# Row-wise absolute maximum of an 8192 x 8192 matrix: loads split over two DMA queues, joins gathered into one, last result transposed on the tensor engine

## Chip, cores and metric

The kernel runs on one core of one Trainium2 chip. The metric is device time in microseconds (us) from launch to end of one execution; lower is better. Before the change the median of 10 runs is 631.82 us (631.76 to 632.32).

## Reference

```python
x = np.random.randn(8192, 8192).astype(np.float32)

def reference(x):
    return np.linalg.norm(x, ord=np.inf, axis=1)
```

The reference takes, for each row of x, the largest absolute value of 8192 float32 numbers. The input is 268.4 MB, the output 32 KB. There is no arithmetic beyond one maximum for each element.

## The kernel before

The 8192 rows of x are handled as 64 "rows" of 128 partitions: one such row is 128 x 8192 numbers (4 MB), one x-row per partition. From here on "row" means such a block of 128 x-rows, and a "pair" is two of them, loaded by one instruction as 128 x 16384 (8 MB).

`PIECES` lists the loads, unit by unit: four single rows (`HEAD`), 23 whole pairs, five pairs cut into pieces, three single rows cut into pieces, and the last row cut into six pieces that shrink from 1984 to 832 columns. Pairs are numbered 1 to 28 here, in the order of loading: pairs 1 to 23 are whole, pair 24 is two loads of 8192, pairs 25 to 28 are cut unevenly. All loads are issued by SyncE (SP, line 106), and land in one buffer, `ring`, of three pairs' width (`RING`); only the last piece has a buffer of its own (`last`). The place in the ring goes round, so pair n lies where pair n-3 lay: its load may start only when VectorE has reduced pair n-3.

VectorE (DVE) does all the reducing (`absmax`, line 58), in the order of the loads. A piece that holds a whole row goes straight to a column of `res`; pieces of rows go to columns of `part`, and `join` (line 63) takes the maximum of a row's columns once they are all there. A join is held back by one reduction (`pending`), so it never stands directly behind the reduction whose result it needs. There are eight joins.

The results stand one per partition, and the output needs them along a line. Rows of results are therefore transposed on TensorE (lines 71 and 82), copied out of PSUM by ScalarE (ACT, lines 72 and 83) and stored from ACT's DMA queue (lines 73 and 84): the four heads once they are first possible, the 28 pairs after the first cut single row, the three single rows near the end. The very last row goes another way: its reduction `fin` (line 108) fills column 0 of a 128 x 32 tile, VectorE transposes that in blocks of 32 x 32 (line 144), and SP stores four lines of 32 numbers (line 145).

The Tile layer that records the kernel adds the semaphore waits and decides, within each engine, in which order instructions stand. DMA completions are counted on eight semaphores, here called lanes 0 to 7, that are given out in turn.

Of the kernel before, what the change touches and what calls it, by code (L numbers as in the profile page):

```python
# [1 line left out]

# [5 lines left out]

P = 128
FP32 = mybir.dt.float32  # L10
MAX = mybir.AluOpType.max

HEAD = 4
PAIRS = 28
PIECES = (
    [[8192]] * HEAD
    + [[16384]] * 23  # L20
    + [[8192, 8192], [12288, 4096], [8960, 7424], [8704, 7680], [5504, 6016, 4864]]
    + [[4288, 3904], [3072, 2752, 2368], [2240, 2112, 1984, 1856]]
    + [[1984, 1664, 1472, 1152, 1088, 832]]
)
RING = 3 * 16384


@with_exitstack
def kernel(
    ctx: ExitStack,  # L30
    tc: tile.TileContext,
    x: bass.AP,
    out: bass.AP,
):
    nc = tc.nc
    n_rows, n_cols = x.shape
    R = n_rows // P
    assert R == 64 and n_cols == 8192

    single = ctx.enter_context(tc.tile_pool(name="single", bufs=1))  # L40
    psum_pool = ctx.enter_context(tc.tile_pool(name="psum", bufs=1, space=bass.MemoryType.PSUM))

    ring = single.tile([P, RING], FP32)
    res = single.tile([P, R], FP32)
    part = single.tile([P, R, 8], FP32)
    ident = single.tile([P, P], FP32)
    make_identity(nc, ident)


    n_last = len(PIECES[-1]) - 1  # L50
    w_last = PIECES[-1][-1]
    last = single.tile([P, w_last + n_last], FP32)
    fin = single.tile([P, 32], FP32)
    fin_t = single.tile([P, 32], FP32)
    nc.gpsimd.memset(fin, 0.0)  # L55

    def absmax(dst, src):
        nc.vector.tensor_reduce(  # L58
            out=dst, in_=src, axis=mybir.AxisListType.X, op=MAX, apply_absolute_value=True,
        )  # L60

    def join(row, n):
        nc.vector.tensor_reduce(  # L63
            out=res[:, row : row + 1], in_=part[:, row, :n], axis=mybir.AxisListType.X, op=MAX,
        )

    def rows_out(r0, n):

        ps = psum_pool.tile([n, P], FP32, name=f"ps{r0}")
        sb = single.tile([n, P], FP32, name=f"sb{r0}")  # L70
        nc.tensor.transpose(ps, res[:, r0 : r0 + n], ident)  # L71
        nc.scalar.copy(sb, ps)  # L72
        nc.scalar.dma_start(
            out=out[r0 * P : (r0 + n) * P].rearrange("(r p) -> r p", p=P), in_=sb
        )

    def pairs_out():
        sb = single.tile([PAIRS, P, 2], FP32, name="sb_pairs")
        both = res[:, HEAD : HEAD + 2 * PAIRS].rearrange("p (g r) -> p g r", r=2)
        for r in range(2):  # L80
            ps = psum_pool.tile([PAIRS, P], FP32, name=f"ps_pairs{r}")
            nc.tensor.transpose(ps, both[:, :, r], ident)  # L82
            nc.scalar.copy(sb[:, :, r], ps)  # L83
        nc.scalar.dma_start(
            out=out[HEAD * P : (HEAD + 2 * PAIRS) * P].rearrange("(g p r) -> g p r", p=P, r=2),
            in_=sb,
        )

    at = 0
    row = 0  # L90
    pending = None
    for u, widths in enumerate(PIECES):
        k = sum(widths) // n_cols
        src = x[row * P : (row + k) * P].rearrange("(p r) m -> p (r m)", r=k)
        off = 0
        n_part = {}
        for h, w in enumerate(widths):
            final = u == len(PIECES) - 1 and h == n_last
            if final:
                buf = last[:, :w]  # L100
            else:
                if at + w > RING:
                    at = 0
                buf = ring[:, at : at + w]
                at += w
            nc.sync.dma_start(out=buf, in_=src[:, off : off + w])
            if final:
                absmax(fin[:, :1], last)
                break
            s = 0  # L110
            while s < w:
                r = row + (off + s) // n_cols
                left = n_cols - (off + s) % n_cols
                if left == n_cols and w - s >= n_cols:
                    c = (w - s) // n_cols
                    absmax(
                        res[:, r : r + c],
                        buf[:, s : s + c * n_cols].rearrange("p (c m) -> p c m", m=n_cols),
                    )
                    s += c * n_cols  # L120
                    continue
                e = min(w, s + left)
                i = n_part.get(r, 0)
                n_part[r] = i + 1
                if r == R - 1:
                    absmax(last[:, w_last + i : w_last + i + 1], buf[:, s:e])
                else:
                    absmax(part[:, r, i : i + 1], buf[:, s:e])

                if pending is not None:  # L130
                    join(*pending)
                    pending = None
                if e - s == left and r < R - 1:
                    pending = (r, i + 1)
                s = e
            off += w
        row += k
        if row == HEAD + 2 * PAIRS + 1:
            pairs_out()
            rows_out(0, HEAD)  # L140
    assert pending is None
    rows_out(HEAD + 2 * PAIRS, R - 1 - HEAD - 2 * PAIRS)

    nc.vector.transpose(fin_t, fin)  # L144
    nc.sync.dma_start(
        out=out[(R - 1) * P :].rearrange("(b c) -> b c", c=32), in_=fin_t[0:P:32, :]
    )
    assert row == R


# [1 line left out]
_INS = ['x']  # L152
_OUTS = [((8192,), 'float32')]


# [23 lines left out]
```

## Time and profile before

| | before |
|---|---|
| median of 10 runs | 631.82 us |
| the profiled execution | 631.78 us |
| its span (first to last instruction) | 630.0 us |
| VectorE busy | 553.5 us (88%) |
| HBM read | 268.44 MB, 426 GB/s over the span |
| TensorE, ScalarE, GpSimd busy | 1.5, 2.3, 0.8 us |

The span is 1.8 us shorter than the time of the same execution. All instants below are microseconds from the start of the span. In rows of the profile, `res<-ring 128x2 f32<-128x16384 f32` is an instruction that reads a tile of 128 partitions by 16384 numbers in `ring` and writes 128 x 2 numbers to `res`; `SPq` rows are the time in which SP's queue was issuing loads or waiting to.

### The profile page before, as it was taken

What the parts mean: (1) busy time and instruction counts of PE and PEld (TensorE: products, weight loads), DVE (VectorE), ACT (ScalarE), POOL (GpSimd) and SP (SyncE); (2) the same over time, 40 slices, a digit from 0 to 9 for tenths busy, and PEclk for the clock granted to TensorE, in tenths of its full rate; (3) what the DMA queues carried; (4) which work ended last, traced back from release to release, by engine and by line L of the source; (5) the groups of instructions that cost most, each with busy time, mean ns of one, the idle gap of its engine ahead of it and who ended that gap; (6) DMA issues with size and microseconds to landing.
All of it is one profiled execution on the core that took longest, in us unless ns stands there. A gap on an engine that the chain in (4) does not pass through costs nothing. (4 is left out here: it accounts for less than half of the span.)

```text
span 630.0 us, 225 instructions
## 1 busy us (share of the span) xinstructions
PE 1.5 (0%) x4; PEld 0.4 (0%) x4; DVE 553.5 (88%) x66; ACT 2.3 (0%) x5; POOL 0.8 (0%) x7
## 2 busy tenths in 40 slices
PE   0000000000000000000000000000000000000000
PEld 0000000000000000000000000000000000000000
DVE  1983988889988889888899888898888999999998
ACT  0000000000000000000000000000000000000000
POOL 0000000000000000000000000000000000000000
DMA  8999999999999999999999999999999999999995
GB/s 370 435 460 420 445 424 441 445 420 449 416 454 412 466 399 466 399 466 399 466 399 466 399 466 399 466 399 466 399 466 399 433 433 424 447 416 428 425 421 237
DMA packets 7698, 268.49 MB, mean 426 GB/s; under 512 B 877, under 2 KB 912, under 8 KB 1936
## 3 DMA queue, kind: packets, MB, share of 16 engines
q1 hardware_dynamic: 7640, 268.44, 98.9%
q10 hardware_dynamic: 56, 0.03, 0.0%
q14 instruction: 2, 0.02, 0.0%
HBM read 268.44 MB, written 0.03 MB: 426 GB/s over the span
## 5 line engine op out<-in xcount | busy, mean ns | idle before, releaser
L58 DVE TENSOR_REDUCE res<-ring 128x2 f32<-128x16384 f32 (+1 forms) x32 | 473.9, 14818 | 73.5 <-DMA ring<-in_x_dram 73.5
L58 DVE TENSOR_REDUCE part<-ring 128x1 f32<-128x4096 f32 (+17 forms) x19 | 70.0, 3735 | 0.0
L58 DVE TENSOR_REDUCE last<-ring 128x1 f32<-128x1984 f32 (+4 forms) x5 | 8.1, 1678 | 0.0
L83 ACT COPY sb_pairs<-ps_pairs 28x128 f32<-28x128 f32 x2 | 0.5, 262 | 540.1 <-PE ps_pairs L82 540.1
L82 PE MATMUL ps_pairs<-ident,res 128*28 128x128 f32 x2 | 0.8, 396 | 539.8 <-DVE res L63 539.8
L63 DVE TENSOR_REDUCE res<-part 128x1 f32<-128x2 f32 (+2 forms) x8 | 1.2, 154 | 0.2
L72 ACT ACT_TABLE_LOAD x1 | 1.3, 1283 | 0.7 <-PEq L163 0.7
L58 DVE TENSOR_REDUCE fin<-last 128x1 f32<-128x837 f32 x1 | 1.0, 1025 | 0.1
L71 PE MATMUL ps<-ident,res 128*4 128x128 f32 (+1 forms) x2 | 0.7, 372 | 77.1 <-DVE res L58 50.8
L72 ACT COPY sb<-ps 4x128 f32<-4x128 f32 (+1 forms) x2 | 0.5, 254 | 75.6 <-PE ps L71 75.6
L82 PEld LDWEIGHTS ps_pairs<-ident,res 128*28 128x28 f32 x2 | 0.2, 104 | 540.4 <-DVE res L63 540.4
masks.py:199 POOL TENSOR_SCALAR_AFFINE_SELECT ident<-ident 128x128 f32<-128x128 f32 x1 | 0.3, 292 | 0.0
L144 DVE STREAM_TRANSPOSE fin_t<-fin 128x32 f32<-128x32 f32 x1 | 0.2, 211 | 0.0
L71 PEld LDWEIGHTS ps<-ident,res 128*4 128x4 f32 (+1 forms) x2 | 0.2, 82 | 77.4 <-issue 50.8
masks.py:197 POOL MEMSET ident<- 128x128 f32 x1 | 0.2, 204 | 0.3 <-POOLq L163 0.3
L55 POOL MEMSET fin<- 128x32 f32 x1 | 0.1, 125 | 0.0
L163 POOL MEMSET const-bfloat16-1.0<- 128x1 bf16 x1 | 0.1, 101 | 0.0
L163 POOL MEMSET const-uint8-127<- 128x1 uint8 x1 | 0.1, 101 | 0.0
L163 POOL MEMSET const-float32-0.0<- 128x1 f32 x1 | 0.1, 98 | 0.2 <-issue 0.2
L163 POOL MEMSET const-float32-1.0<- 128x1 f32 x1 | 0.1, 98 | 0.0
## 6 DMA issues: line engine op xcount, KB each, us to landing
ring<-in_x_dram SPq DMA_DIRECT2D x6, 4096.0 KB, 30.9
ring<-in_x_dram SPq DMA_DIRECT2D x1, 6144.0 KB, 36.1
ring<-in_x_dram SPq DMA_DIRECT2D x1, 4480.0 KB
ring<-in_x_dram SPq DMA_DIRECT2D x1, 4352.0 KB, 34.2
ring<-in_x_dram SPq DMA_DIRECT2D x1, 3840.0 KB
ring<-in_x_dram SPq DMA_DIRECT2D x1, 3712.0 KB
ring<-in_x_dram SPq DMA_DIRECT2D x1, 3008.0 KB
ring<-in_x_dram SPq DMA_DIRECT2D x1, 2752.0 KB, 41.3
```

Of the source, the lines that this page charges most:

```text
L55: nc.gpsimd.memset(fin, 0.0)
L58: nc.vector.tensor_reduce(out=dst, in_=src, axis=mybir.AxisListType.X, op=MAX, apply_absolute_value=True,)
L63: nc.vector.tensor_reduce(out=res[:, row : row + 1], in_=part[:, row, :n], axis=mybir.AxisListType.X, op=MAX,)
L71: nc.tensor.transpose(ps, res[:, r0 : r0 + n], ident)
L72: nc.scalar.copy(sb, ps)
L82: nc.tensor.transpose(ps, both[:, :, r], ident)
L83: nc.scalar.copy(sb[:, :, r], ps)
L144: nc.vector.transpose(fin_t, fin)
L163: nc = _bacc.Bacc("TRN2", target_bir_lowering=False, num_devices=1)
```

## The change

- The first 24 loads (4 heads and pairs 1 to 20) stay on SP; pairs 21 to 28, the three single rows and the last row are issued by ScalarE (ACT). On ACT, all these loads stand ahead of the copies and stores. Every load is put behind what its own engine already has (`keep_in_program_order`).
- Rows are renumbered: pairs take rows 0 to 55 of x, the seven single rows (the four heads included) rows 56 to 62. One transpose, one copy and one store serve the seven.
- All rows from number 48 (`CUT`) on have four columns in `part` (15 x 4 columns), and those not written by a reduction are zeroed beforehand. One instruction joins all 15 rows, directly before the last row.
- The pieces of pairs 25 to 28, of the three single rows and of the last row have other widths; their number is unchanged.
- The zeroing of `part`, and the building of the identity matrix, now wait until the first row is reduced. They were ahead of it.
- The last row's result is transposed on TensorE, copied out of PSUM by VectorE and stored by SP as one line of 128 numbers.

```diff
-    + [[8192, 8192], [12288, 4096], [8960, 7424], [8704, 7680], [5504, 6016, 4864]]
-    + [[4288, 3904], [3072, 2752, 2368], [2240, 2112, 1984, 1856]]
-    + [[1984, 1664, 1472, 1152, 1088, 832]]
+    + [[8192, 8192], [7232, 9152], [6720, 9664], [8640, 7744], [5568, 5568, 5248]]
+    + [[4480, 3712], [3392, 1920, 2880], [2752, 1600, 2048, 1792]]
+    + [[1792, 1664, 1472, 1280, 1088, 896]]
 )
+SP_PAIRS = 20
+CUT = 48
+K = 4
...
+    def setup(after):
+        for ins in (nc.gpsimd.memset(part[:, :, 1:], 0.0), nc.gpsimd.memset(ident, 0.0)):
+            tc.add_manual_dep(
+                ins.ins, after.name,
+                mybir.DependencyInfo(mybir.DependencyClass.Sync, mybir.DependencyReason.DATA),
+                reason="not before the first row is in",
+            )
+        make_identity(nc, ident, nomemset=True)
...
+        if k == 2:
+            row, next_pair = next_pair, next_pair + 2
+        else:
+            row, next_one = next_one, next_one + 1
...
-            nc.sync.dma_start(out=buf, in_=src[:, off : off + w])
+            queue = nc.sync if u < HEAD + SP_PAIRS else nc.scalar
+            tc.keep_in_program_order(
+                queue.dma_start(out=buf, in_=src[:, off : off + w])
+            )
...
-                if pending is not None:
-                    join(*pending)
-                    pending = None
-                if e - s == left and r < R - 1:
-                    pending = (r, i + 1)
...
+        if u == len(PIECES) - 2:
+            nc.vector.tensor_reduce(
+                out=res[:, CUT:], in_=part, axis=mybir.AxisListType.X, op=MAX,
+            )
+    pairs_out()
+    singles_out()
+    fin_ps = psum_pool.tile([1, P], FP32)
+    fin_sb = single.tile([1, P], FP32)
+    nc.tensor.transpose(fin_ps, fin, ident)
+    nc.vector.tensor_copy(out=fin_sb, in_=fin_ps)
+    nc.sync.dma_start(out=out[(R - 1) * P :].rearrange("(r p) -> r p", p=P), in_=fin_sb)
```

What the Tile layer makes of this around the handover, in the order of each engine's instructions in the built program ("waits DVE 22" means that VectorE's first 22 reductions are done; heads are VectorE's reductions 1 to 4):

```
SP    load pair 19 -> place 3 of the ring, lane 6, waits DVE 20 (pair 16)
SP    load pair 20 -> place 1 of the ring, lane 0, waits DVE 21 (pair 17)
ACT   load pair 21 -> place 2 of the ring, lane 7, waits DVE 22 (pair 18)
ACT   load pair 22 -> place 3 of the ring, lane 1, waits DVE 23 (pair 19)
ACT   load pair 23 -> place 1 of the ring, lane 2, waits DVE 25
ACT   loads of pair 24, lanes 3 and 4
DVE   reduction 22: place 2, waits lane 5      (pair 18)
DVE   reduction 23: place 3, waits lane 6      (pair 19)
DVE   reduction 24: place 2, waits lane 7      (pair 21)
DVE   reduction 25: place 1, waits lane 0      (pair 20)
DVE   reduction 26: place 3, waits lane 1      (pair 22)
```

In the kernel before, reduction 24 is pair 20's, reduction 25 is pair 21's, and the load of pair 23 waits for DVE 24.

## Prediction

> **What bounds the kernel now.** I read the page first: span, slices, and the costliest group of VectorE.
>
> ```profile
> span 630.0 us, 225 instructions
> ...
> DVE  1983988889988889888899888898888999999998
> ...
> DMA  8999999999999999999999999999999999999995
> ...
> L58 DVE TENSOR_REDUCE res<-ring 128x2 f32<-128x16384 f32 (+1 forms) x32 | 473.9, 14818 | 73.5 <-DMA ring<-in_x_dram 73.5
> ```
>
> The DMA engines are full in every slice but the last, and VectorE's 73.5 us of idle time all end on a load landing. So the loads bound the kernel; but from slice 32 to 39 VectorE is at 9, so the last fifth has another limit. The timeline of VectorE shows both:
>
> ```profile
> 12.88 8.69 DVE L58 TENSOR_REDUCE res<-ring 128x1 f32<-128x8192 f32 x1 [12.88 <-DMA ring<-in_x_dram]
> 22.56 8.69 DVE L58 TENSOR_REDUCE res<-ring 128x1 f32<-128x8192 f32 x1 [1.00 <-DMA ring<-in_x_dram]
> ...
> 390.32 17.22 DVE L58 TENSOR_REDUCE res<-ring 128x2 f32<-128x16384 f32 x1 [2.13 <-DMA ring<-in_x_dram]
> 409.67 17.22 DVE L58 TENSOR_REDUCE res<-ring 128x2 f32<-128x16384 f32 x1 [2.13 <-DMA ring<-in_x_dram]
> ...
> 448.40 17.22 DVE L58 TENSOR_REDUCE res<-ring 128x2 f32<-128x16384 f32 x1 [2.14 <-DMA ring<-in_x_dram]
> 467.74 17.22 DVE L58 TENSOR_REDUCE res<-ring 128x2 f32<-128x16384 f32 x1 [2.12 <-DMA ring<-in_x_dram]
> 487.11 17.22 DVE L58 TENSOR_REDUCE res<-ring 128x2 f32<-128x16384 f32 x1 [2.14 <-DMA ring<-in_x_dram]
> ```
>
> The whole pair at 487.11 is pair 23, so 390.32 is pair 18. A pair arrives every 19.36 us and costs VectorE 17.22, which leaves 2.14 idle. From 487.11 on there is no idle time: the tail is cut so that pieces lie ready when VectorE comes to them. The end of the timeline:
>
> ```profile
> 591.21 0.15 DVE L63 TENSOR_REDUCE res<-part 128x1 f32<-128x2 f32 x1
> 591.28 8.73 DVE L58 TENSOR_REDUCE part<-ring 128x1 f32<-128x4288 f32 x2
> 591.42 0.11 PEld L82 LDWEIGHTS ps_pairs<-ident,res 128*28 128x28 f32 x1 [5.21 <-DVE res L63]
> 591.42 0.40 PE L82 MATMUL ps_pairs<-ident,res 128*28 128x128 f32 x1 [4.92 <-DVE res L63]
> 591.86 0.26 ACT L83 COPY sb_pairs<-ps_pairs 28x128 f32<-28x128 f32 x1 [5.06 <-PE ps_pairs L82]
> ...
> 626.14 1.02 DVE L58 TENSOR_REDUCE fin<-last 128x1 f32<-128x837 f32 x1
> 627.20 0.21 DVE L144 STREAM_TRANSPOSE fin_t<-fin 128x32 f32<-128x32 f32 x1
> 627.44 0.66 SPq L145 DMA_DIRECT2D out_dram<-fin_t  x1
> ```
>
> The last load is issued at 612.41 and takes 12.3 us to land (issues of DMA), so 624.7, before `fin` starts at 626.14. Two rules follow: time taken off VectorE after 487.11 comes off the end, up to about 1.4 us; and **any idle time that VectorE gains before 487.11 goes to the end in full**, since nothing behind it has slack.
>
> **What the Trainium skill says.** "DMA: Bandwidth & Descriptors", section "Issuing engines are not separate DMA queues": loads from SP and ACT run on the same 16 DMA engines and interleave; a second issuer saves only issue time. Issue time is no limit here: SP stands waiting, and one issue takes 0.33 us against 19.36 of transfer. The same page, "Queues, rings and completion order": each DMA engine works round robin through the queues that have work, packet by packet, and one queue's descriptors are taken in ring order. In the trace of before only ACT's tiny stores ever meet the loads, so no number there shows it for large transfers. "TensorE: Matmul & The Clock Gate", "Part 4: PE-mode transpose": the output goes to PSUM, so a copy must follow; lines 82 and 83 show this pair at 0.40 and 0.26 us.
>
> **The handover, step by step.** The built program fixes two things: SP issues pair 20 and ACT pair 21 independently, and VectorE reduces 21 ahead of 20. Pair 23's load waits for both, because pair 20's place is the one it takes.
>
> 1. Up to here nothing differs. Pair 18 is reduced 390.32 to 407.54, pair 19 lands at 409.67 and is reduced to 426.89. Pair 20's load is issued at 388.2 (when 17 was done), pair 21's at 407.57.
> 2. What an issue costs on empty queues: SP's first load is issued at 0.74, lands at 12.88, the next 9.68 later; so 12.14 - 9.68 = 2.46 us beyond the transfer. Part lies ahead of the first byte, part behind the last; only their sum matters. Pair 21's data can start 2.46 us after its issue less the part at the end, pair 20's when pair 19's has passed; seen as landings these are 410.03 and 409.67. Pair 20 leads by 0.36 us.
> 3. Before, pair 20 then had the engines alone and landed at 429.0. Now two queues of equal rows share. 2 x 19.36 = 38.72 us of transfer are under way, and both land near the end of it, pair 21 at 409.67 + 38.72 = 448.39. Its own landing is unmoved from before; it is pair 20 that is 19 us late.
> 4. VectorE waits for pair 21 from 426.89 to 448.39: 21.5 us idle. Then 21 runs to 465.6, and 20 to 482.8. Had 20 been first, its place would be free at 465.6.
> 5. Pair 22 was issued at 426.9 and lands at 467.74 as before. Behind it ACT has pair 23, held until 482.8, and in its queue behind that the loads of pair 24 and all others. So the **DMA engines run dry** for 482.8 + 2.46 - 467.74 = 17.5 us. Pair 23 lands at 482.8 + 2.46 + 19.36 = 504.65 instead of 487.11: **+17.5 us**. VectorE reduces 22 from 482.8 to 500.0 and waits 4.6. Cross-check by idle time: 2.14 + 21.5 + 4.6 = 28.2 before the tail, against 5 x 2.14 = 10.7.
> 6. From pair 23 on the state is that of before, 17.5 us later: VectorE starts it as it lands, and pair 24 is queued behind it. ACT's copies and stores stand behind its loads, but no load stands behind a copy.
>
> **The tail.** Reductions over ring pieces after 487.11 number the same, over the same elements, and the last row's six cover the same 8192. Eight joins go. One costs the chain 0.15 us: 538.86 - 530.02 = 8.84 for two of 4096 with a join behind, against the 4.41 each less the 0.08 by which neighbours overlap (8.73 for two merged), 8.69 start to start. So -1.2 us. One join of 15 x 4 comes: from 512 elements at 676 ns and 8192 at 8681, an element costs 1.04 ns and an instruction 142; 60 elements are 0.20, and as it stands directly behind its last input I add the 0.10 of idle time that `fin` shows in that position: +0.30 (0.2 to 0.5). Sum -0.9.
>
> Do the new pieces starve VectorE? At 1.182 ns per column (19.36 / 16384), with pair 23's landing as zero, pair 26's 9664 lands at 58.1 and is wanted at 58.9; the 8640 of pair 27 at 68.3, wanted at 69.1; the last piece at 135.5, wanted at 138.1. The smallest margin is 0.8, so I add nothing, but up to +1 in the range.
>
> **After the last reduction.** Line 144's 0.21, begun 0.02 after `fin`, goes. In come the step to TensorE (0.05), the matmul (0.37, line 71), the step to VectorE (0.04) and a copy of 128 numbers out of PSUM, whose VectorE price no row shows: ScalarE's copies take 0.25, a VectorE instruction of 128 elements by the slope 0.275. 0.05 + 0.37 + 0.04 + 0.27 - 0.23 = **+0.5** (0.3 to 0.8). The store is one line of 128 instead of four of 32, with 2.6 us from `fin_t` to the end of the span; kept at that, +-0.3.
>
> **At nothing.** GpSimd's memsets and identity move from 0.7 to about 22; they are wanted first in pair 25's reductions, 480 us later. The table load (1.28, ACT) moves behind the last load's issue, where ACT has nothing else. The heads' store at 51.5 merges with that of the singles: issued near 637, some 7 us before the last store at 645, behind the loads in ACT's own queue. Without that cover it would cost its own landing, about 2.6. Renumbered rows move the same bytes.
>
> **Sum.** Profiled execution: 631.78 + 17.5 - 0.9 + 0.5 = 648.9. The median of before is 0.04 above that execution, so 648.9 for the median too.
>
> **The rivals.**
> - *Unequal shares* (0.10). If ACT's queue gets 60%, pair 21 lands at 410.03 + 19.36 / 0.6 = 442.3, but pair 22, behind it, keeps slowing 20, which lands near 458.4. VectorE does 21 to 459.5, 20 to 476.7; pair 23 lands at 498.5, +11.4: about 642.8. Below 50% pair 21 lands no later than 448.4, as all work is done by then.
> - *The engines take whole transfers in turn* (0.04). Then pair 21 comes alone, landing at 429.4; 20 follows, at 448.4, under the reduction of 21 (to 446.6). 20 is done at 465.6, pair 23 issued 2.1 before 22 lands, against 2.46 needed: +0.35. The total is 631.8 + 0.3 - 0.9 + 0.5 = 631.7, no change. The point from which it decides: pair 21 must land by about 431 with pair 20 ready by 448. Nothing in the trace excludes it; the skill's packet-wise turn speaks against it.
> - *Two streams slow each other* (0.05). If 38.7 us of shared transfer run 10% below the 433 GB/s of one stream, 21 lands 3.9 later: 652.8.
> - *The handover is harmless*, and only joins and transpose count: 631.4; with the table load gone from the start and no stores among the loads it could be 630. I leave 0.01: the built order excludes it, unless waits cost nothing.
>
> **Chances.** Equal sharing has 0.80; its own range is 646.5 to 650.5 (2.46 +-0.8 for the restart, +1 for the tail, +-0.5 for the end). A run of this kernel can tell about 0.2% (1.3 us) from no change. Slower 0.95, within 0.2% 0.04, faster 0.01. The range 643.8 to 651.2 takes in part of unequal shares and of the slower stream.
>
> **What would show it.** Right: before the tail one idle stretch of VectorE of about 21.5 us ending on a landing near 448.4, then two pairs back to back; a hole in DMA of some 17 us around 470 to 485; pair 23 starting near 504.7; one join of about 0.2 us; a matmul and a copy between `fin` and the last store; no new idle time in the tail. Wrong: pair 21 landing near 429 or 442, DMA at 9 in all slices, or new waits in the tail of over 1 us.

## The result and the profile after

| | before | after |
|---|---|---|
| median | 631.88 us (29 runs) | 648.27 us (8 runs, 648.12 to 648.69) |
| ratio after / before | | 1.0259 (95% interval 1.025 to 1.0268) |
| profiled execution, its span | 631.78, 630.0 us | 648.44, 646.7 us |
| VectorE busy | 553.5 us | 552.5 us |

The change made the kernel 16.4 us slower; the forecast was 648.9 us. VectorE works no longer than before, so the time went into waiting. The page of the kernel after shows where (slices of 16.2 us; the digits are tenths busy):

```profile
span 646.7 us, 218 instructions
...
DVE  1893898888898888898888898842999799999998
...
DMA  9999999999999998999999999999718999999996
...
L63 DVE TENSOR_REDUCE res<-ring 128x2 f32<-128x16384 f32 (+1 forms) x25 | 413.1, 16535 | 75.6 <-DMA ring<-in_x_dram 75.6
L63 DVE TENSOR_REDUCE part<-ring 128x1 f32<-128x8192 f32 (+19 forms) x26 | 130.0, 5072 | 16.1 <-DMA ring<-in_x_dram 16.1
```

Two notches stand side by side: VectorE falls to 4 and 2 (slices 27 and 28), and two slices later the DMA row, at 8 or 9 everywhere else but in the last slice, falls to 7 and 1. VectorE is starved first, the DMA engines afterwards. Idle time of VectorE is 75.6 + 16.1 = 91.7 us against 73.5 before, 18.2 more. The timeline of VectorE and of the issues around the handover:

```profile
388.32 0.33 SPq L120 DMA_DIRECT2D ring<-in_x_dram  x1
390.43 17.22 DVE L63 TENSOR_REDUCE res<-ring 128x2 f32<-128x16384 f32 x1 [2.13 <-DMA ring<-in_x_dram]
407.68 218.02 ACTq L120 DMA_DIRECT2D ring<-in_x_dram  x28
409.77 17.22 DVE L63 TENSOR_REDUCE res<-ring 128x2 f32<-128x16384 f32 x1 [2.12 <-DMA ring<-in_x_dram]
448.65 51.47 DVE L63 TENSOR_REDUCE res<-ring 128x2 f32<-128x16384 f32 x3 [21.66 <-DMA ring<-in_x_dram]
505.08 34.41 DVE L63 TENSOR_REDUCE res<-ring 128x2 f32<-128x16384 f32 x3 [4.96 <-DMA ring<-in_x_dram]
539.40 95.27 DVE L63 TENSOR_REDUCE part<-ring 128x1 f32<-128x7232 f32 x22
```

The row at 390.43 is pair 18, at 409.77 pair 19. Then VectorE idles for 21.66 us. The row at 448.65 merges three reductions: pairs 21, 20 and 22. It is idle once more for 4.96 us until pair 23, at 505.08 instead of 487.11, and then never waits for a load again. The chain of work that ended last names what pair 23 waited for (start, us, what):

```profile
448.65 34.36 DVE res L63 x2
483.01 0.02 issue
483.03 22.03 DMA ring<-in_x_dram
505.05 0.02 issue
505.08 34.41 DVE res L63 x3
```

Pairs 21 and 20 had to be reduced (34.36 us), only then was pair 23's load issued, and it took 22.03 us to land: 19.36 of transfer and 2.67 for the start on empty queues. The view by windows (stretch, length, busy us and counts of PE, PEld, DVE, ACT, POOL, clock, DMA share, GB/s) shows the hole in the loads:

```profile
448.00:467.00 19.00, 0.00 (x0) 0.00 (x0) 18.35 (x2) 0.00 (x0) 0.00 (x0) 1.00 0.91 393
467.00:486.00 19.00, 0.00 (x0) 0.00 (x0) 19.00 (x2) 0.00 (x0) 0.00 (x0) 1.00 0.16 55
486.00:505.00 19.00, 0.00 (x0) 0.00 (x0) 14.12 (x1) 0.00 (x0) 0.00 (x0) 1.00 0.96 414
```

From 467 to 486 VectorE is fully busy and the DMA engines carry 55 GB/s. The end of the timeline, for the joins and the last row:

```profile
634.71 0.22 DVE L149 TENSOR_REDUCE res<-part 128x15 f32<-128x60 f32 x1
634.84 7.98 DVE L63 TENSOR_REDUCE last<-ring 128x1 f32<-128x1792 f32 x5
...
642.85 1.09 DVE L63 TENSOR_REDUCE fin<-last 128x1 f32<-128x901 f32 x1
644.00 0.08 PEld L157 LDWEIGHTS fin_ps<-ident,fin 128*1 128x1 f32 x1 [8.63 <-DVE fin L63]
644.00 0.37 PE L157 MATMUL fin_ps<-ident,fin 128*1 128x128 f32 x1 [8.13 <-DVE fin L63]
644.41 0.28 DVE L158 COPY fin_sb<-fin_ps 1x128 f32<-1x128 f32 x1 [0.46 <-PE fin_ps L157]
644.71 0.32 SPq L159 DMA_DIRECT2D out_dram<-fin_sb  x1
```

The difference of the two spans, 16.7 us, is the sum of five terms read from the two timelines: pair 23 starts 17.97 later (505.08 against 487.11); from there to `fin` 1.26 less (137.77 against 139.03); `fin` itself 0.07 more; from its end to the last store's issue 0.49 more (0.77 against 0.28); from that issue to the end of the span 0.57 less (1.99 against 2.56).

### The profile page after: what moved, and what is told of

The parts are those of the page before. It is cut to its first block, busy times and chain, and to the rows that moved or that the text cites. A ratio compares the mean times of both kernels' runs of the same rounds, so it can differ in the third digit from the quotient of the medians.

```text
span 646.7 us, 218 instructions
## 1 busy us (share of the span) xinstructions
PE 1.2 (0%) x4; PEld 0.3 (0%) x4; DVE 552.5 (85%) x59; ACT 2.0 (0%) x4; POOL 0.8 (0%) x7
## 4 chain that ended last, share of the span: by engine, by line
DMA 55%; DVE 44%; issue 1%; SPq 0%; PE 0%
DMA ring<-in_x_dram 55%; DVE res L63 27%; DVE part L63 16%; DVE last L63 1%; SPq L120 0%; DVE fin L63 0%; PE fin_ps L157 0%; DVE fin_sb L158 0%; DVE res L149 0%
## 5 line engine op out<-in xcount | busy, mean ns | idle before, releaser
L63 DVE TENSOR_REDUCE res<-ring 128x2 f32<-128x16384 f32 (+1 forms) x25 | 413.1, 16535 | 75.6 <-DMA ring<-in_x_dram 75.6
L63 DVE TENSOR_REDUCE part<-ring 128x1 f32<-128x8192 f32 (+19 forms) x26 | 130.0, 5072 | 16.1 <-DMA ring<-in_x_dram 16.1
L63 DVE TENSOR_REDUCE last<-ring 128x1 f32<-128x1792 f32 (+4 forms) x5 | 8.0, 1662 | 0.0
```

What stands on the lines that cost most here:

```text
L63: return nc.vector.tensor_reduce(out=dst, in_=src, axis=mybir.AxisListType.X, op=MAX, apply_absolute_value=True,).ins
```

## Experiments

The theory on trial: the small edits save about 1.3 us, and all of the loss comes from the handover of the loads from SP to ACT. Two causes lie in it: the two queues share the DMA engines, so that pair 20 lands late, and VectorE's order puts pair 21 ahead of pair 20, so that pair 23's load is held back. The main rivals were that sharing alone does it, that the order alone does it, and that ACT is a worse issuer.

### The changed kernel on one queue

```diff
-SP_PAIRS = 20
+SP_PAIRS = 99
```

> The changed kernel with all loads on SP; everything else of the change stays (one join, new pieces, last row through TensorE). Theory (the handover alone made it slower): pair 21 is reduced after pair 20, no hole in the loads, and what is left are the small terms read from the trace of the changed kernel: tail -1.26, last reduction +0.07, TensorE step +0.49, single-line store -0.57, so 631.9 - 1.3 = 630.6 us. Rival (the new pieces or the renumbered rows cost something as well): above 632.

Measured: 630.66 us (14 runs), ratio to before 0.9978 (0.997 to 0.9986). All the loss is gone with the second queue, and the rest of the change gains 1.3 us. The timeline from pair 22 on (pair 22, pair 23 with pair 24, the pieces, the join) has no wait after pair 23, and pair 23 is where it was before:

```profile
468.01 17.22 DVE L63 TENSOR_REDUCE res<-ring 128x2 f32<-128x16384 f32 x1 [2.14 <-DMA ring<-in_x_dram]
487.35 34.41 DVE L63 TENSOR_REDUCE res<-ring 128x2 f32<-128x16384 f32 x3 [2.13 <-DMA ring<-in_x_dram]
521.68 95.27 DVE L63 TENSOR_REDUCE part<-ring 128x1 f32<-128x7232 f32 x22
616.98 0.22 DVE L149 TENSOR_REDUCE res<-part 128x15 f32<-128x60 f32 x1
```

### Every load on ACT

```diff
-SP_PAIRS = 20
+SP_PAIRS = -HEAD
```

> The changed kernel with every load on ACT and none on SP: one queue again, the other one. Theory (what costs is the sharing and the order at the handover, not who issues): 630.7, as one_queue. Rival (ACT issues slower or its queue carries less): 632 or more.

Measured: 630.76 us (13 runs), ratio 0.998 (0.9972 to 0.9988), within 0.1 us of the version with all loads on SP. Who issues the loads makes no difference that these runs can tell. ACT is not the cause; having two queues is.

### Two queues, reductions in the order of the loads

```diff
-        return nc.vector.tensor_reduce(
+        return tc.keep_in_program_order(nc.vector.tensor_reduce(
             out=dst, in_=src, axis=mybir.AxisListType.X, op=MAX, apply_absolute_value=True,
-        ).ins
+        )).ins
```

> The changed kernel with its two queues, but VectorE's reductions are kept in the order of the loads, so pair 20 is reduced ahead of pair 21. Theory (two queues share the DMA engines by halves, so pair 20 lands 19 us late): VectorE idles 21.5 us before pair 20, lands of pair 20 and 21 both near 448.5; pair 23 is issued at 465.7, before pair 22 lands, so the hole in the loads is gone (0.4 at most), but VectorE enters the tail 12.6 us late and cannot catch up, since the tail has no idle time: 630.6 + 12.9 = 643.5. Rival A (the swapped order alone is the cause): 630.6 to 631. Rival B (the engines take whole transfers in turn): pair 20 lands at 429 or 448 alone, 631 or a loss of about 2.5.

Measured: 643.33 us (4 runs), ratio 1.0179 (1.0162 to 1.0196). The timeline of VectorE (pair 19, then pairs 20 to 24 in one merged row, then the pieces) and the window of the former hole:

```profile
409.87 17.22 DVE L63 TENSOR_REDUCE res<-ring 128x2 f32<-128x16384 f32 x1 [2.13 <-DMA ring<-in_x_dram]
448.58 85.78 DVE L63 TENSOR_REDUCE res<-ring 128x2 f32<-128x16384 f32 x6 [21.48 <-DMA ring<-in_x_dram]
534.28 95.26 DVE L63 TENSOR_REDUCE part<-ring 128x1 f32<-128x7232 f32 x22
```

```profile
467.00:486.00 19.00, 0.00 (x0) 0.00 (x0) 19.00 (x2) 0.00 (x0) 0.00 (x0) 1.00 1.01 428
```

Pair 20 is now first in line and still comes no earlier than 448.58: on one queue it would have been 429. The trace has the two landings 0.2 us apart. So the queues share by halves, and transfers are not taken whole. The DMA records of the changed kernel say the same: those that start between 416 and 444 us hold 6.3 MB on each of the two queues. The hole is gone (428 GB/s where the changed kernel has 55). Pair 23, issued at 465.83, lands at 488.82, which is 1.6 us later than pair 22's landing at 467.90 and 19.36 of transfer give, and not 0.4; VectorE is behind and does not notice. Yet 12.7 us are lost against one queue: VectorE was idle for 21.5 us and has work without a pause from then to the end, so it cannot make up for it. Sharing by itself costs 12.7 us here, without any hole in the loads.

### One queue, pairs 20 and 21 reduced in the wrong order

The diff shows the swap alone; the run also has `SP_PAIRS = 99` and the `keep_in_program_order` of the experiment before.

```diff
+                    if u == HEAD + 19:
+                        held = todo
+                    else:
+                        absmax(*todo)
+                    if u == HEAD + 20:
+                        absmax(*held)
```

> All loads on SP, in order, but VectorE reduces pair 21 ahead of pair 20. Theory: pair 20 lands at 429 but waits for its turn until pair 21 has landed at 448.4 and is reduced, so pair 23 is issued as late as in the changed kernel: idle 21.5 us, hole of 17 us, 648.2. Rival (sharing is the cause, the order harmless): about 630.6 or 631.

Measured: 648.24 us (4 runs), ratio 1.0256 (1.0241 to 1.0272), the time of the changed kernel. Its timeline is that of the changed kernel too:

```profile
448.82 51.47 DVE L63 TENSOR_REDUCE res<-ring 128x2 f32<-128x16384 f32 x3 [21.48 <-DMA ring<-in_x_dram]
505.17 34.41 DVE L63 TENSOR_REDUCE res<-ring 128x2 f32<-128x16384 f32 x3 [4.88 <-DMA ring<-in_x_dram]
```

The order alone suffices for the whole loss of 17.6 us. The two causes do not add: once VectorE waits for pair 21, which lands at the same time with one queue or two, it no longer matters that pair 20 is late as well.

### The handover at pair 4, with the reductions in order and without

```diff
-SP_PAIRS = 20
+SP_PAIRS = 3
```

In order (with the edit of the third experiment):

> Two queues, reductions kept in order, but the handover comes 17 pairs earlier: SP has the heads and pairs 1 to 3, ACT all others. Theory: sharing makes VectorE late by 12.6 us once more, but VectorE gains 2.14 us on every later pair and has caught up after six; the loads lose only the 0.4 us by which pair 6's issue comes too late: 631.0. Rival (two queues cost transfer time themselves, or ACT is the slower issuer): 633 or more.

With the order that the Tile layer chooses:

> As early_in_order, with the reductions left to the Tile layer, which again puts the first pair of ACT (4) ahead of the last of SP (3). Theory: the hole in the loads is lost transfer time and is not caught up, so the loss is the same as late in the kernel: 648.2. Rival (the loss is VectorE's lateness, which is caught up over 20 pairs): 631 to 633.

Measured: 633.09 us (20 runs, 631.82 to 633.95; ratio 1.0017, 1.001 to 1.0023) in order, 648.59 us (4 runs; ratio 1.0262, 1.0246 to 1.0277) swapped. The swapped one confirms that a hole in the loads is not made up for here, even with 20 pairs to go. In order, VectorE's lateness is indeed caught up, as its timeline shows (pairs 2, 3 to 10, 11, 12):

```profile
80.84 17.22 DVE L63 TENSOR_REDUCE res<-ring 128x2 f32<-128x16384 f32 x1 [2.13 <-DMA ring<-in_x_dram]
119.54 137.10 DVE L63 TENSOR_REDUCE res<-ring 128x2 f32<-128x16384 f32 x8 [21.48 <-DMA ring<-in_x_dram]
256.91 17.22 DVE L63 TENSOR_REDUCE res<-ring 128x2 f32<-128x16384 f32 x1 [0.27 <-DMA ring<-in_x_dram]
276.26 17.22 DVE L63 TENSOR_REDUCE res<-ring 128x2 f32<-128x16384 f32 x1 [2.13 <-DMA ring<-in_x_dram]
```

Eight pairs follow without a pause, then the usual 2.13 us are back. But 2.4 us are lost against one queue where 0.3 to 0.4 were expected, and 633.09 is what the rival said. Pair 11 stands at 256.91, and nine periods of 19.35 after pair 2 would be 255.0: the loads themselves have lost 1.9 us. By the landings in the trace it happens at pair 6, which is issued 2.1 us before pair 5 has landed and comes 1.7 us late. The trace has 16 partial completions for each load; from first to last they are 0.6 us apart before, about 1.7 from then on and 2.3 in the tail. In the tail VectorE has to wait once more, 0.24 us at 558.25, and comes to `fin` 2.2 us later than on one queue. The price of 2.46 us for a start on empty queues does not give the 1.7 us at pair 6. As for the rival: ACT alone issues as well as SP (630.76), most loads after pair 6 land 19.35 us apart as on one queue, and the next experiment has such a loss without a second queue.

### A load issued just before its queue runs dry, on one queue

`late_once` makes the load of pair 10 wait for pair 8's reduction instead of pair 7's; `late_ten` does so for pairs 6 to 15 (`if HEAD + 5 <= u < HEAD + 15`). Both are otherwise the changed kernel on one queue; the diff does not show the lines that keep the reductions' names for it.

```diff
+            if u == HEAD + 9:
+                tc.add_manual_dep(
+                    load.ins, reduced[u - 2],
+                    mybir.DependencyInfo(mybir.DependencyClass.Sync, mybir.DependencyReason.DATA),
+                    reason="only when the pair two back is reduced",
+                )
```

> As one_queue, but the load of pair 10 waits for pair 8 to be reduced, not 7, so that it is issued 2.1 us before the queue ahead of it has landed. In the kernel with two queues and an early handover this situation came up once, and its pair landed 1.7 us late where the price of a start on empty queues (2.46 + transfer) gives 0.3. Theory A (a start just before the queue runs dry costs more than one on empty queues): pair 10 lands 1.7 late, 632.3. Theory B (the extra came from the two queues): 0.3 late, 631.0.

> As late_once, but for pairs 6 to 15, ten times. If P is the time by which an issue has to come ahead of the last landing, every second of these loads is P - 2.14 late (one that is late leaves the next more time). Theory A (P near 3.8): 5 x 1.7 = 8.3, 639. Theory B (P = 2.46): 5 x 0.3 = 1.6, 632.3.

Measured: 632.96 us (16 runs, 631.55 to 633.42; ratio 1.0013, 1.0006 to 1.0021) for one such load, 642.76 us (4 runs, 640.95 to 643.27; ratio 1.0165, 1.0151 to 1.0179) for ten. Theory B is out in both, so the two queues are not needed for the extra cost. Theory A has the direction, but both sizes are larger than it said: 2.3 against 1.7, and 12.1 against 8.3. The timeline of `late_once` (pairs 8, 9, 10, 11):

```profile
197.19 17.22 DVE L63 TENSOR_REDUCE res<-ring 128x2 f32<-128x16384 f32 x1 [2.13 <-DMA ring<-in_x_dram]
216.54 17.22 DVE L63 TENSOR_REDUCE res<-ring 128x2 f32<-128x16384 f32 x1 [2.13 <-DMA ring<-in_x_dram]
238.45 17.22 DVE L63 TENSOR_REDUCE res<-ring 128x2 f32<-128x16384 f32 x1 [4.70 <-DMA ring<-in_x_dram]
257.80 17.22 DVE L63 TENSOR_REDUCE res<-ring 128x2 f32<-128x16384 f32 x1 [2.13 <-DMA ring<-in_x_dram]
```

Pair 8 is done at 214.41 and pair 10 starts at 238.45, 24.04 us later: 4.7 us beyond its 19.36 of transfer. But 2.1 us of these passed while pair 9 was still landing, until 216.5. What the loads lose is the rest, 2.6 us, and that is what a start on empty queues costs (2.46 in the kernel before, 2.67 at pair 23 of the changed kernel). So the 2.1 us by which the load was issued ahead gained nothing, where the expectation let them count in full. At this load the first of the 16 partial completions is 0.7 us late and the last 2.6; their spread goes from 0.8 to 2.7 us and stays there for all loads that follow.

In the profiled execution of `late_ten` (640.95 us) it is not every second load that is late. Pairs 6, 8, 10 and 13, issued 2.1 to 2.25 us before the landing ahead of them, landed 2.4, 2.8, 1.3 and 2.8 us late; the six others, issued 2.4 to 4.9 us ahead, at most 0.4. The spread goes up and down there and is back at 0.5 us by pair 15, so it does not always stay. Why the head start is lost is not settled by these runs.

### The handover alone, in the kernel before

```diff
-            nc.sync.dma_start(out=buf, in_=src[:, off : off + w])
+            queue = nc.sync if u < HEAD + 20 else nc.scalar
+            tc.keep_in_program_order(
+                queue.dma_start(out=buf, in_=src[:, off : off + w])
+            )
```

> The kernel before with the handover alone: loads of pair 21 and later on ACT, everything else as it was. The Tile layer again reduces pair 21 ahead of pair 20. Theory: +18.0 as in the changed kernel, and about 1.1 more, because here ACT's two copies of the pairs' results stand in front of the second single row's loads and wait for a join near 609 (591 in the trace of before, 18 later), when the loads ahead have 2.4 us left: 632.0 + 18.0 + 1 = 650 to 651. Rival (something else in the change makes it slow): 632.

Measured: 650.59 us (4 runs, 649.43 to 651.11), ratio 1.0288 (1.0272 to 1.0304). In the profile pair 23 starts at 505.06, as in the changed kernel, and `fin` at 645.18: 140.12 us from one to the other against 139.03 before, the 1.1 us foretold for the copies in front of loads on ACT. The timeline has the copy at 609.82 with the loads following it at 609.88 and 610.73:

```profile
609.82 0.26 ACT L83 COPY sb_pairs<-ps_pairs 28x128 f32<-28x128 f32 x1 [5.05 <-PE ps_pairs L82]
609.88 0.34 ACTq L108 DMA_DIRECT2D ring<-in_x_dram  x1
610.31 0.38 ACTq L84 DMA_DIRECT2D out_dram<-sb_pairs  x1
610.73 16.99 ACTq L108 DMA_DIRECT2D ring<-in_x_dram  x11
```

So moving all copies and stores behind the loads, as the full change does, is what spares it this; the loss at the handover needs nothing else of the change.

### The small edits

The widths of the kernel before, on one queue:

```diff
-    + [[8192, 8192], [7232, 9152], [6720, 9664], [8640, 7744], [5568, 5568, 5248]]
...
+    + [[8192, 8192], [12288, 4096], [8960, 7424], [8704, 7680], [5504, 6016, 4864]]
...
```

> As one_queue, but with the widths of the pieces of the kernel before. Theory: with the joins gone VectorE comes to the old pieces 1.2 us earlier and has to wait for some; the last landing (624.7 in the trace of before) then sets the end: 630.6 to 631.1. Rival (recutting is worth nothing): 630.6, no idle time in the tail.

The last row transposed on VectorE, on one queue (and a `fin` of 128 x 32 again, zeroed with the identity):

```diff
-    nc.tensor.transpose(fin_ps, fin, ident)
-    nc.vector.tensor_copy(out=fin_sb, in_=fin_ps)
-    nc.sync.dma_start(out=out[(R - 1) * P :].rearrange("(r p) -> r p", p=P), in_=fin_sb)
+    nc.vector.transpose(fin_t, fin)
+    nc.sync.dma_start(
+        out=out[(R - 1) * P :].rearrange("(b c) -> b c", c=32), in_=fin_t[0:P:32, :]
+    )
```

> As one_queue, but the last row is transposed on VectorE in 32 x 32 blocks and stored as four lines of 32, as in the kernel before. Theory: it gives back 0.49 of TensorE's step and loses the 0.57 of the store, so 630.7, within 0.2 of one_queue. Rival (the store's shorter end in the changed kernel had to do with SP's queue being idle and not with its form): 630.1.

The opposite edit in the kernel before:

> The kernel before with only the last row's way out changed: TensorE, copy by VectorE, one line of 128. Theory (trace of the changed kernel: chain +0.49, store -0.57): 631.8, no change. Rival (the step of the prediction, with the store unchanged): 632.4.

Measured: 630.60 us with the old widths (12 runs; ratio 0.9978, 0.997 to 0.9987), 630.72 us with the transpose on VectorE (13 runs; ratio 0.998, 0.9972 to 0.9988), 631.85 us for TensorE in the kernel before (13 runs; ratio 0.9999, 0.9991 to 1.0007). Recutting is worth nothing: with the old widths the tail has no idle time either, so the rival was right there. The two ways out for the last row are equal, in both kernels. The last stores of `dve_last` and of `before_pe_last`:

```profile
626.52 0.65 SPq L158 DMA_DIRECT2D out_dram<-fin_t  x1
627.98 0.32 SPq L146 DMA_DIRECT2D out_dram<-fin_sb  x1
```

With spans of 629.0 and 630.0 us, four lines take 2.5 us from issue to the end and one line 2.0, in either kernel. So it is the form of the store that counts and not an idle queue of SP, which was the rival. The gain of 1.3 us that all three one-queue versions share is put down to the joins: the working of the tail below finds 1.1 us of it there (renumbering and the later setup are in all three and were not tried apart).

## Why the prediction was right

**Steps 1 and 2** (nothing differs up to pair 19; a start costs 2.46 us): pair 19 is at 409.77 against 409.67, the 0.1 being there from the first landing on. The start on empty queues measured 2.67.

**Step 3** (halves, both pairs near 448.4): measured 448.65 in the changed kernel. The kernel with pair 20 first in line shows that both land there, 20 at 448.55 and 21 at 448.75. These landings exclude unequal shares (442.3 and 458.4), whole transfers in turn (429.4) and streams 10% slower (over 452; the sum there should have added 4.3 us, not 3.9).

**Step 4** (21.5 us idle, 20 done at 482.8): 21.66 idle, done at 483.01. **Step 5** (hole of 17.5, pair 23 at 504.65, wait of 4.6): pair 23 at 505.08, wait of 4.96; the term is 17.97 instead of 17.5, of which 0.1 is the start of the run and about 0.2 each the landing of pair 21 and the dearer restart. **Step 6** (no further loss): no wait for a load up to `fin`. It was close: the smallest margin was forecast at 0.8 us, and one piece of pair 27 landed at 582.85 and was taken at 583.01.

The prediction used both causes and did not say what each was worth. The runs do: sharing alone 12.7 us, the order alone 17.6, both 17.6.

**The tail**, -0.9, was 0.4 too small: measured -1.26. The price of the joins that go was too low. The first of them, in the kernel before:

```profile
530.02 8.73 DVE L58 TENSOR_REDUCE part<-ring 128x1 f32<-128x4096 f32 x2
538.79 0.15 DVE L63 TENSOR_REDUCE res<-part 128x1 f32<-128x2 f32 x1
538.86 8.68 DVE L58 TENSOR_REDUCE res<-ring 128x1 f32<-128x8192 f32 x1
```

The two reductions end at 538.75. Without the join the next one would start 0.08 before that, as neighbours do, at 538.67; it starts at 538.86, so the join costs 0.19. The prediction had 0.15, because it took 8.69 us for the two without a join where 8.73 less 0.08 is 8.65. Seven of the eight cost 0.19, one (at 585.91) only 0.06, together 1.4 us instead of 1.2. The new join costs 0.25 by the same count (the reductions before it end at 634.67, the next starts at 634.84), not 0.30. That makes -1.14. Of the rest, 0.06 is idle time in front of `fin`, 0.10 before and 0.04 after; the other 0.06 stays open. `fin`, 0.07 longer by its wider input, was left out of the sum.

**After the last reduction**, +0.5: measured +0.49. The term that failed is the store, kept at nothing: one line of 128 numbers is 0.57 us sooner from issue to the end than four lines of 32; 0.34 of that is the issue itself (0.32 us against 0.66). That cancels TensorE's step, which the run of the kernel before with that edit alone confirms (631.85). Tail and store together are 0.9 us better than forecast, the handover 0.4 and `fin` 0.1 worse; hence 648.44 in the profiled execution instead of 648.9. The path was the one foretold; that the total came within 0.5 us owes something to these errors, which partly cancel.

## What to carry to other kernels

When loads for one ordered consumer are handed from one DMA queue to another, the last loads of the old queue and the first of the new one run side by side at half rate, and the one needed first comes late; in a tail without slack that lateness stays. Look at the built order on the consumer as well. The Tile layer swapped it in all three kernels here that had loads on two queues and left the reductions free, and in none with one queue (these runs do not show why). Where the loads bound the kernel, a ring buffer turns the swap into a hole in the loads that later slack does not give back. Issue a load well before the queue ahead of it runs dry: 2.1 us ahead of the last landing was too late here, and cost as much as a start on empty queues.

## What the runs showed of the hardware that was not expected

- A load of 8 MB issued 2.1 us before its queue had landed came 2.6 us late, about as late as one issued on empty queues only when the last load has landed (2.46 to 2.67). The 16 partial completions of a load spread from 0.8 to 2.7 us with it and kept that spread to the end of the loads; in the run with ten such loads the spread shrank again. Runs of such kernels also scatter more: 631.55 to 633.42 us, against 630.5 to 630.87 without such a load (`late_once` and `one_queue`).
- A store of one line of 512 bytes ended the span 1.99 us after its issue, one of four lines of 128 bytes 2.56 us; the issue took 0.32 us in one case and 0.66 in the other.
- A join of 15 x 4 numbers takes VectorE 0.22 us and costs the chain 0.25, little more than a join of two numbers (0.15 and 0.19).
